# A mixture-of-experts router that reads the residual rows themselves, block by block

## The chip, the cores and the metric

The kernel runs on one core of a Trainium2 chip. The metric is the device time of one execution in microseconds (us). The engines are TensorE (PE, with its weight loads as PEld), VectorE (DVE), ScalarE (ACT), GpSimd (POOL) and SyncE (SP); SP, ACT and POOL issue the DMAs. The trace comes from one profiled execution, with times counted from the start of its span.

## The reference, cut to what matters

One layer of a hybrid encoder on 1024 rows of 1024 channels: a linear-recurrence branch and a differential attention, merged, then cross-attention to 256 memory rows, then a mixture of experts. The change touches the step from the cross-attention's output to the first expert.

```
x = x + MemCrossAttn(RMSNorm(x), RMSNorm(mem))
h = x * rsqrt(mean(x*x) + 1e-6) * norm_ffn                # one row factor, one gain per channel
gp = softmax(h @ w_group + b_group)                       # 4 groups
gval, gidx = top_k(gp, 1)
el = (h @ w_router + b_router)[8 experts of group gidx]   # 32 experts in all
ev, eidx = top_k(el, 2);  ew = softmax(ev) * gval
# each row goes to its two experts: y = (silu(h @ Wg) * (h @ Wu)) @ Wd
x = x + sum over the two experts of ew * y
```

## The kernel before, in words

Rows are worked on in eight blocks of 128 (tb). Matrix products keep float32 accuracy by splitting each operand into a rounded part and a remainder: ScalarE writes the rounded part, VectorE the difference (`split`), and `mm3` issues three matmuls. Weight pieces of 512 KB come from HBM in a fixed order through class `Weights` (L45): `load` issues the DMAs on SP, `split_one` makes the two parts (L97 on ScalarE, L101 on VectorE), `prefetch(n)` allows n pieces in flight ahead, and `after` ties an instruction behind another in the planner's order. All large tiles share one pool of 51 slots of 4 KB per partition (`slot`). PSUM has four one-bank tiles (`bank`) and two two-bank tiles (`bank2`), eight banks in all.

The memory attention runs as a list of steps written by hand, `SEQ` (L1226), one letter and a block or pair each: P, T, S, A, O and M make queries, scores, probabilities and their products with the memory values; C (L1004) is the output projection into PSUM; N (L1020) adds it to x, starts x's write to the output, squares and sums the row on ScalarE (L1027), lets POOL make the row factor (a power of -0.5), multiplies x by factor and gain on VectorE (L1037, tile n3) and writes the normalised row to DRAM (h3_d) from ScalarE's queue. R (L1044) transposes a block of n3 with PE and splits it, two PSUM tiles of four transposes each. L (L1058) multiplies two blocks at once, 256 columns, with the router weights `wrs` (36 logits as a rounded part and a remainder side by side, 72 columns), and ScalarE adds the bias. l (L1070) transposes the logits back, adding the two halves by the matrix id2, and VectorE copies them to SBUF. r and q are the two halves of `st_route` (L1116): r picks group and experts into one-hot rows `ohf` and a mask `mb`; q counts each row's rank among the rows of its expert with PE (prk), makes the gate weights, and then the values and rank one-hots. f is a call of `prefetch`. The list ends with C7 N7 R6 f4 l2 R7 q1 L3 l3 r2 q2; r2 and q2 route blocks 4 to 7. `rt` (L1080) packs small router tiles into shared slots of 1024 numbers.

After the list, PE multiplies one-hots by values into a table of row numbers (pTi) and one of gate weights (pTw), 96 places for each expert (L1280). `table` (L1287) converts row numbers to int32 (idx, L1289) on VectorE; POOL gathers the 96 rows of the first expert from h3_d by an indirect DMA (L1301, tile xe); they are transposed (pxe) and the expert's matmuls (pgu, py) begin. Each of the 32 experts takes twelve weight pieces and scatters its result by an indirect DMA that adds to the output. Before the first gather four weight pieces are split.

A planner that runs a timeline model decides each engine's order of instructions from program order and dependencies.

Of the kernel before, what the change touches and what calls it, by code (L numbers as in the profile page):

```python
# [20 lines left out]
T = 1024  # L21
# [110 lines left out]
def block_kernel(ctx, tc, a):  # L132
# [13 lines left out]
    def slot(name, dt=F32, shape=(P, 1024)):  # L146
        return S.tile(list(shape), dt, tag="s", name=name)

    def bank(name, dt=F32, shape=(P, 512)):
        return pb1.tile(list(shape), dt, tag="b1", name=name)  # L150
# [4 lines left out]
    def f(x):  # L155
        return x.bitcast(F32)
# [53 lines left out]
    rowt = slot("row")  # L210
    row = rowt[:, 0:NROW]
    nc.gpsimd.dma_start(row, a["row"].to_broadcast([P, NROW]))
    posi = cp.tile([P, NB], I32, name="posi")
    nc.gpsimd.dma_start(posi, a["pos"])
    ident = cp.tile([P, P], F32, name="ident")
# [8 lines left out]
    def rstd_of(ss, n, cnt, name):  # L224

        t = sm.tile([P, 16], F32, tag="rs0", name=name + "m")
        r = sm.tile([P, 16], F32, tag="rs1", name=name + "r")
        G.tensor_scalar(t[:, :n], ss, 1.0 / cnt, EPS, op0=OP.mult, op1=OP.add)
        G.tensor_tensor(r[:, :n], t[:, :n], negh[:, :n], op=OP.pow)
        return r  # L230
# [96 lines left out]
    def split(src, h, l):  # L327
        A.activation(h, src, AF.Copy)
        V.tensor_tensor(l, src, f(h), op=OP.subtract)  # L329
# [571 lines left out]
    wr = slot("wr", F32, (P, 8, 36))  # L901
    wrs = slot("wrs", F32R, (P, 8, 72))
    nc.sync.dma_start(wr, a["w_r"])
    A.activation(wrs[:, :, 0:36], wr, AF.Copy)
    V.tensor_tensor(wrs[:, :, 36:72], wr, f(wrs[:, :, 0:36]), op=OP.subtract)

# [111 lines left out]
        return ps if tb >= NB - HN else [both]  # L1018

    def st_N(tb, ps):  # L1020
        x, t = x1[tb], slot(f"n3_{tb}")
        ss = sm.tile([P, 16], F32, tag="ss", name=f"n3_{tb}s")
        n = len(ps)
        parts = [slice(i * D // n, (i + 1) * D // n) for i in range(n)]
        for i, c in enumerate(parts):
            V.tensor_tensor(x[:, c], x[:, c], ps[i], op=OP.add)
            A.activation(t[:, c], x[:, c], AF.Square, accum_out=ss[:, i:i + 1])  # L1027
        nc.scalar.dma_start(a["out"][tb * P:(tb + 1) * P, :], x)
        if n == 2:
            m, r = (sm.tile([P, 16], F32, tag=f"rs{i}", name=f"n3_{tb}r{i}") for i in range(2))  # L1030
            G.tensor_scalar(ss[:, 0:1], ss[:, 0:1], 1.0, D * EPS, op0=OP.mult, op1=OP.add)
            G.tensor_scalar(m[:, 0:1], ss[:, 1:2], ss[:, 0:1], 1.0 / D, op0=OP.add, op1=OP.mult)
            G.tensor_tensor(r[:, 0:1], m[:, 0:1], negh[:, 0:1], op=OP.pow)
        else:
            r = rstd_of(ss[:, 0:1], 1, D, f"n3_{tb}")
        for c in parts:
            V.scalar_tensor_tensor(t[:, c], x[:, c], r[:, 0:1], gffn[:, c], op0=OP.mult, op1=OP.mult)  # L1037
        h3[tb] = t
        nc.scalar.dma_start(h3_d[tb * P:(tb + 1) * P, :], t)
        x1[tb] = None  # L1040

    h3T, lgT = {}, {}

    def st_R(tb):  # L1044

        src = h3.pop(tb)
        c = slice((tb % 2) * P, (tb % 2) * P + P)
        for kq in range(2):
            ps = bank(f"ph3T{tb}_{kq}", F32, (P, 4, P))
            for kk_ in range(4):  # L1050
                k = 4 * kq + kk_
                E.transpose(ps[:, kk_, :], src[:, k * P:(k + 1) * P], ident)  # L1052
            if tb % 2 == 0:
                h3T[tb // 2, kq] = [slot(f"h3T{tb}_{kq}_{i}", F32R, (P, 4, 256)) for i in range(2)]
            t = h3T[tb // 2, kq]
            split(ps, t[0][:, :, c], t[1][:, :, c])

    def st_L(g):  # L1058

        pl = bank(f"plog{g}", F32, (P, 256))[0:72]  # L1060
        for k in range(8):
            t = h3T[g, k // 4]
            for i in range(2):
                W.last = E.matmul(pl, wrs[:, k, :], t[i][:, k % 4, :], start=k + i == 0, stop=k + i == 8)  # L1064
            if k % 4 == 3:
                del h3T[g, k // 4]
        lgT[g] = slot(f"lgT{g}", F32, (P, 256))[0:72]
        A.activation(lgT[g], pl, AF.Identity, bias=vec[0:72, C_BR:C_BR + 1])

    def st_l(g):  # L1070
        src = lgT.pop(g)
        pt = bank(f"plgT{g}", F32, (P, 2, 36))
        for j in range(2):
            W.last = E.matmul(pt[:, j, :], src[:, j * P:(j + 1) * P], id2, start=True, stop=True)  # L1074
        V.tensor_copy(lg[:, 2 * g:2 * g + 2, :], pt)


    rpool = {}
# [1 line left out]
    def rt(name, *shape, dt=F32):  # L1080

        n = math.prod(shape)
        if dt not in rpool or rpool[dt][1] + n > 1024:
            rpool[dt] = [slot(name, dt), 0]
        t, o = rpool[dt]
        rpool[dt][1] = o + n
        v = t[:, o:o + n]
        if len(shape) > 1:
            names = "abcd"[:len(shape)]
            v = v.rearrange(f"p ({' '.join(names)}) -> p {' '.join(names)}", **dict(zip(names, shape)))  # L1090
        return v
# [13 lines left out]
    V.memset(onesb, 1.0)  # L1105
    ohf = rt("ohf", 2, NB, 32)
    mb = cp.tile([P, NB, 32], BF, name="mb")
    lgf = rt("lg", NB * 36)
    lg = lgf.rearrange("p (a b) -> p a b", a=NB)
    rk, ew, ewl = rt("rk", 2, NB), rt("ew", 2, NB), rt("ewl", 2, NB)  # L1110
    ewh = sm.tile([P, 2, NB], F32R, name="ewh", bufs=1)
# [4 lines left out]
    def st_route(b0, n2):  # L1116
# [51 lines left out]
        for t in range(n2 - 1):  # L1168
            E.matmul(prk[:, t + 1:, :], onesb, mb[:, b0 + t:b0 + t + 1, :].to_broadcast([P, n2 - 1 - t, 32]),
                     start=False, stop=t == n2 - 2)  # L1170

        V.tensor_reduce(sg, gd, axis=AX.X, op=OP.add)
        V.reciprocal(gval, sg)
        V.tensor_tensor(m2, m2, m1, op=OP.subtract)
        A.activation(m2, m2, AF.Exp)
        V.tensor_scalar(dn, m2, 1.0, None, op0=OP.add)
        V.reciprocal(dn, dn)
        V.tensor_tensor(ew[:, 0, bs], dn, gval, op=OP.mult)
        V.tensor_tensor(ew[:, 1, bs], ew[:, 0, bs], m2, op=OP.mult)
        V.tensor_copy(ewh[:, :, bs], ew[:, :, bs])  # L1180
        V.tensor_tensor(ewl[:, :, bs], ew[:, :, bs], f(ewh[:, :, bs]), op=OP.subtract)
        va = rt(f"vals{b0}", 2, n2, 3, 32, dt=F32R)
        oh = rt(f"ohs{b0}", 2, n2, CAP, dt=F32R)

        def value(i, c):
            V.tensor_tensor(va[:, :, :, i, :], ohf[:, :, bs], c[:, :, bs, None].to_broadcast([P, 2, n2, 32]),  # L1186
                            op=OP.mult)
# [6 lines left out]
        for k in range(2):  # L1194
            V.tensor_tensor(oh[:, k], slots[:, None, :].to_broadcast([P, n2, CAP]),  # L1195
                            rk[:, k, bs, None].to_broadcast([P, n2, CAP]), op=OP.is_equal)
        value(1, f(ewh))
        value(2, ewl)
        coded.append([(oh[:, k, t, :], va[:, k, t]) for k in range(2) for t in range(n2)])
# [8 lines left out]
    for hf in range(2):  # L1208
        w = W.take(4)
        for tb in range(NB):  # L1210
# [11 lines left out]

    wcq, wco = W.take(4), None
    NG_ = NB // 2
    PF = 12,20,28,36,41
    SEQ = ("P0 T0 P1 T1 S0 S1 P2 P3 O00 O01 O02 T2 O03 T3 M00 M01 C0 A2 S2 S3 N0 C1 N1 P4 O10 O11 P5 "  # L1226
# [3 lines left out]
    done = set()  # L1230
    routes = [st_route(0, 2), st_route(2, 2), st_route(4, 4)]
    pco = {}
    for op in SEQ.split():
        kind, n = op[0], int(op[1])
        if kind == "P":
            st_P(n)
            if n == NB - 1:
                wcq = None
        elif kind == "T":
            st_T(n)  # L1240
        elif kind == "S":
            st_S(n)
        elif kind == "A":
            st_A(n)
        elif kind == "O":
            st_O(n, (int(op[2]),))
        elif kind == "M":
            st_M(n, int(op[2]))
        elif kind == "C":
            if wco is None:  # L1250
                wco = W.take(4)
                W.split_ahead = 0
            pco[n] = st_C(n)
            if n % 2 == 1 and n - 1 in done or n % 2 == 0 and n + 1 in done:
                del om[n // 2]
            done.add(n)
        elif kind == "N":
            st_N(n, pco.pop(n))
        elif kind == "R":
            st_R(n)  # L1260
        elif kind == "L":
            st_L(n)
        elif kind == "l":
            st_l(n)
        elif kind == "w":
            for _ in range(n):
                W.split_one()
        elif kind == "f":
            W.prefetch(PF[n])
        else:  # L1270
            last = W.last
            next(routes[n])
# [13 lines left out]

    def table(code, parts, w_, ix):  # L1287

        V.tensor_scalar(ix, code, 2.0 * T, None, op0=OP.add)  # L1289
        V.tensor_copy(w_, parts[:, 0])  # L1290
        V.tensor_tensor(w_, w_, parts[:, 1], op=OP.add)

    wts = cp.tile([P, 32], F32, name="wts")[0:CAP]
    idx = cp.tile([P, 32], I32, name="idx")[0:CAP]
    table(pTi, pTw, wts, idx)

    xe = slot("xe")[0:CAP]
    G.memset(xe, 0.0)
# [223 lines left out]
```

## Time and profile before

| | us |
|---|---|
| median of 3 runs (lowest, highest) | 1950.39 (1950.25, 1954.46) |
| the profiled execution | 1948.1 |
| its span | 1946.3 |
| PE busy | 1868.9 (96%) |
| DVE busy | 1296.6 (67%) |
| ACT busy | 1103.5 (57%) |
| POOL busy | 327.8 (17%) |

A busy share is an average over the span. The page's row of 40 slices shows that PE is at nine tenths or more in nearly all of them, except the first, the last and the one that begins at 1314 us, between routing and experts. The granted clock of TensorE over the whole run is 0.987 of full speed. The weight DMAs of the experts fill the DMA engines from about 1370 us to the end.

### The profile page before, as it was taken

What the parts mean: (1) busy time and instruction counts of PE and PEld (TensorE: products, weight loads), DVE (VectorE), ACT (ScalarE), POOL (GpSimd) and SP (SyncE); (2) the same over time, 40 slices, a digit from 0 to 9 for tenths busy, and PEclk for the clock granted to TensorE, in tenths of its full rate; (3) what the DMA queues carried; (4) which work ended last, traced back from release to release, by engine and by line L of the source; (5) the groups of instructions that cost most, each with busy time, mean ns of one, the idle gap of its engine ahead of it and who ended that gap; (6) DMA issues with size and microseconds to landing.
All of it is one profiled execution on the core that took longest, in us unless ns stands there. A gap on an engine that the chain in (4) does not pass through costs nothing. (4 is left out here: it accounts for less than half of the span.)

```text
span 1946.3 us, 25814 instructions
## 1 busy us (share of the span) xinstructions
PE 1868.9 (96%) x9214; PEld 1491.7 (77%) x9214; DVE 1296.6 (67%) x1766; ACT 1103.5 (57%) x1631; POOL 327.8 (17%) x432
## 2 busy tenths in 40 slices
PE   6999999999999999899999999996999999999996
PEld 5888888888888888778888887875777777777664
DVE  5222324677777758887444425675899999999985
ACT  5233324555555546876212215452888888888885
POOL 2144430122222221100000001111111111111110
PEclk9999999999999999999999999997999999999998
DMA  5222244433333121225322401177999999999996
GB/s 201 86 87 87 87 134 137 125 108 107 111 118 120 55 101 57 71 90 187 108 77 86 187 22 65 56 281 272 322 355 346 337 349 358 353 348 338 348 367 218
DMA packets 115027, 353.40 MB, mean 182 GB/s; under 512 B 14864, under 2 KB 28304, under 8 KB 114896
## 3 DMA queue, kind: packets, MB, share of 16 engines
q1 hardware_dynamic: 102992, 322.11, 46.9%
q0 software_dynamic: 7296, 17.04, 3.8%
q10 hardware_dynamic: 4608, 12.58, 1.6%
q8 instruction: 73, 1.20, 0.2%
q14 instruction: 58, 0.48, 0.1%
HBM read 311.82 MB, written 48.23 MB: 185 GB/s over the span
## 5 line engine op out<-in xcount | busy, mean ns | idle before, releaser
L101 DVE TENSOR_TENSOR wl<-wraw,wh 128x1024 fp32r<-128x1024 f32 x480 | 576.9, 1227 | 123.7 <-ACT wh L97 111.7
L97 ACT ACTIVATE wh<-wraw 128x1024 fp32r<-128x1024 f32 x480 | 496.3, 1057 | 113.0 <-PE pgu L161 15.9
L160 PE MATMUL pgu<-wl,xeh 128*96 128x512 f32 x512 | 203.7, 398 | 1.0 <-DVE wl L101 1.0
L159 PE MATMUL pgu<-wh,xeh 128*96 128x512 f32 x512 | 203.7, 398 | 0.3 <-ACT wh L97 0.3
L161 PE MATMUL pgu<-wh,xel 128*96 128x512 f32 x512 | 201.2, 393 | 0.0
L505 ACT ACTIVATE p<-pS,st 128x256 f32<-128x256 f32 (+7 forms) x128 | 94.9, 747 | 103.3 <-DVE st L498 51.7
L159 PE MATMUL pga<-hH,wh 128*128 128x512 f32 x320 | 127.4, 398 | 2.5 <-DVE wT L539 2.5
L160 PE MATMUL pga<-hL,wh 128*128 128x512 f32 x320 | 126.0, 394 | 0.0
L161 PE MATMUL pga<-hH,wl 128*128 128x512 f32 x320 | 125.5, 392 | 0.0
L160 PEld LDWEIGHTS pgu<-wl,xeh 128*96 128x96 f32 x512 | 82.9, 162 | 43.5 <-DVE wl L101 12.5
L159 PEld LDWEIGHTS pgu<-wh,xeh 128*96 128x96 f32 x512 | 83.0, 162 | 33.8 <-ACT wh L97 0.5
L161 PEld LDWEIGHTS pgu<-wh,xel 128*96 128x96 f32 x512 | 82.9, 162 | 33.4 <-DVE xel L329 0.2
L1351 POOL DMA_INDIRECT out<-y,idx x32 | 46.4, 1451 | 357.8 <-ACT y L1350 352.9
L514 POOL TENSOR_SCALAR p<-p,st 128x128 f32<-128x128 f32 (+3 forms) x64 | 55.0, 860 | 305.2 <-DVE st L513 159.4
L160 PE MATMUL py<-wl,ah 128*96 128x512 f32 x256 | 101.7, 397 | 0.3 <-DVE wl L101 0.2
L161 PE MATMUL py<-wh,ah 128*96 128x512 f32 x256 | 100.4, 392 | 0.0
L159 PE MATMUL pqk<-wh,hH 128*128 128x512 f32 x256 | 100.3, 392 | 0.0
L161 PE MATMUL pqk<-wh,hL 128*128 128x512 f32 x256 | 100.2, 391 | 0.0
L160 PE MATMUL pqk<-wl,hH 128*128 128x512 f32 x256 | 99.7, 389 | 0.0
L375 ACT ACTIVATE qk<-pT,gq 128x512 f32<-128x512 f32 x32 | 20.2, 686 | 106.8 <-PE pT L374 93.9
L159 PE MATMUL py<-wh,ah 128*96 128x512 f32 x256 | 80.0, 393 | 0.3 <-ACT wh L97 0.3
L493 PE MATMUL pS<-kH,qS 128*128 128x512 f32 (+2 forms) x192 | 69.5, 365 | 5.2 <-ACT p L505 5.2
(527 smaller groups left out, 4415.8 us busy)
## 6 DMA issues: line engine op xcount, KB each, us to landing
wraw<-in_w_gu SPq DMA_DIRECT2D x256, 512.0 KB
wraw<-in_w_dn SPq DMA_DIRECT2D x128, 512.0 KB
wraw<-in_w_cm SPq DMA_DIRECT2D x32, 512.0 KB
x<-in_x SPq DMA_DIRECT2D x16, 512.0 KB
wraw<-in_w_qk SPq DMA_DIRECT2D x32, 256.0 KB
qk_d<-qk SPq DMA_DIRECT2D x32, 256.0 KB
qr<-qk_d SPq DMA_DIRECT2D x32, 256.0 KB
kr<-qk_d SPq DMA_DIRECT2D x32, 256.0 KB
```

The source lines that it names most:

```text
L97: ins = nc.scalar.activation(h, raw, AF.Copy)
L101: nc.vector.tensor_sub(l, raw, h.bitcast(F32))
L159: W.seen(E.matmul(out, lh, rh, start=start, stop=False))
L160: E.matmul(out, lh, rl, start=False, stop=False)
L161: E.matmul(out, ll, rh, start=False, stop=stop)
L375: A.activation(out[i][:, :, c], pt, AF.Copy, scale=gq[:, i:i + 1])
L493: E.matmul(ps[:, o:o + c], lhs, kh_[h, m][:, o:o + c], start=True, stop=False)
L505: A.activation(p[:, :n], ps[:, :n], AF.Exp, bias=mx[:, m:m + 1], accum_out=ls[:, m:m + 1])
L514: G.tensor_scalar(pp[1][:, :n], pp[1][:, :n], rl[:, 1:2], 0.0, op0=OP.mult, op1=OP.add)
L1351: G.indirect_dma_start(out=a["out"][:, :], out_offset=bass.IndirectOffsetOnAxis(ap=dest, axis=0), in_=y, in_offset=None, bounds_check=T - ...
```

## The change

R transposes x itself, as soon as the projection is added, and the channel gains are multiplied into the router weights once, early on; for that a column layout of the gains is read at the start by a POOL DMA. L works on one block of 128 columns, without bias. l multiplies the transposed logits by the row factor and adds the bias row (`brow`, made once by a transpose). N no longer makes the normalised row: a new step H does, for the gather alone, with row factors kept in `r3`. The squares of N go into the projection's own PSUM tile, not into n3. In q the rank part comes ahead of the gate weights. The weight splits in front of the experts are ordered behind the row-number conversion (`W.anchor`). Before the list of steps, a gather of 96 numbers that are all out of bounds is issued, which moves no row. SEQ has the new steps; L and l stand per block, C7 (the last projection) is now followed by l5, H6, N7, q1, L6, R7, l6, L7, H7, l7, r2, f4, q2.

```diff
+    gcol = cp.tile([P, 8], F32, name="gcol")
+    with nc.allow_non_contiguous_dma(reason="1024 gains, one per channel"):
+        nc.gpsimd.dma_start(gcol, a["nffn"].rearrange("o (k p) -> p (o k)", p=P))
...
+    V.tensor_tensor(wr, wr, gcol[:, :, None].to_broadcast([P, 8, 36]), op=OP.mult)
...
     def st_N(tb, ps):
-        x, t = x1[tb], slot(f"n3_{tb}")
+        x = x1[tb]
...
-            A.activation(t[:, c], x[:, c], AF.Square, accum_out=ss[:, i:i + 1])
+            A.activation(ps[i], x[:, c], AF.Square, accum_out=ss[:, i:i + 1])
...
-            m, r = (sm.tile([P, 16], F32, tag=f"rs{i}", name=f"n3_{tb}r{i}") for i in range(2))
+            m = sm.tile([P, 16], F32, tag="rs0", name=f"n3_{tb}r0")
...
-            G.tensor_tensor(r[:, 0:1], m[:, 0:1], negh[:, 0:1], op=OP.pow)
+            G.tensor_tensor(r3[:, tb:tb + 1], m[:, 0:1], negh[:, 0:1], op=OP.pow)
...
-            r = rstd_of(ss[:, 0:1], 1, D, f"n3_{tb}")
-        for c in parts:
-            V.scalar_tensor_tensor(t[:, c], x[:, c], r[:, 0:1], gffn[:, c], op0=OP.mult, op1=OP.mult)
-        h3[tb] = t
+            m = sm.tile([P, 16], F32, tag="rs0", name=f"n3_{tb}r0")
+            G.tensor_scalar(m[:, 0:1], ss[:, 0:1], 1.0 / D, EPS, op0=OP.mult, op1=OP.add)
+            G.tensor_tensor(r3[:, tb:tb + 1], m[:, 0:1], negh[:, 0:1], op=OP.pow)
+    uses = [0] * NB
+    def used(tb):
+        uses[tb] += 1
+        if uses[tb] == 2:
+            x1[tb] = None
+    def st_H(tb):
+        t = slot(f"n3_{tb}")
+        V.scalar_tensor_tensor(t, x1[tb], r3[:, tb:tb + 1], gffn, op0=OP.mult, op1=OP.mult)
...
-        x1[tb] = None
-    h3T, lgT = {}, {}
+        used(tb)
+    xT = {}
...
     def st_R(tb):
...
-        src = h3.pop(tb)
-        c = slice((tb % 2) * P, (tb % 2) * P + P)
...
-            ps = bank(f"ph3T{tb}_{kq}", F32, (P, 4, P))
+            ps = bank(f"pxT{tb}_{kq}", F32, (P, 4, P))
...
-                E.transpose(ps[:, kk_, :], src[:, k * P:(k + 1) * P], ident)
-            if tb % 2 == 0:
-                h3T[tb // 2, kq] = [slot(f"h3T{tb}_{kq}_{i}", F32R, (P, 4, 256)) for i in range(2)]
-            t = h3T[tb // 2, kq]
-            split(ps, t[0][:, :, c], t[1][:, :, c])
-    def st_L(g):
-        pl = bank(f"plog{g}", F32, (P, 256))[0:72]
+                E.transpose(ps[:, kk_, :], x1[tb][:, k * P:(k + 1) * P], ident)
+            t = xT[tb, kq] = slot(f"xT{tb}_{kq}", F32R, (P, 2, 4, P))
+            split(ps, t[:, 0], t[:, 1])
+        used(tb)
+    def st_L(tb):
+        pl = bank(f"plog{tb}", F32, (P, P))[0:72]
         for k in range(8):
-            t = h3T[g, k // 4]
+            t = xT[tb, k // 4]
...
-                W.last = E.matmul(pl, wrs[:, k, :], t[i][:, k % 4, :], start=k + i == 0, stop=k + i == 8)
+                W.last = E.matmul(pl, wrs[:, k, :], t[:, i, k % 4, :], start=k + i == 0, stop=k + i == 8)
...
-                del h3T[g, k // 4]
-        lgT[g] = slot(f"lgT{g}", F32, (P, 256))[0:72]
-        A.activation(lgT[g], pl, AF.Identity, bias=vec[0:72, C_BR:C_BR + 1])
-    def st_l(g):
-        src = lgT.pop(g)
-        pt = bank(f"plgT{g}", F32, (P, 2, 36))
-        for j in range(2):
-            W.last = E.matmul(pt[:, j, :], src[:, j * P:(j + 1) * P], id2, start=True, stop=True)
-        V.tensor_copy(lg[:, 2 * g:2 * g + 2, :], pt)
+                del xT[tb, k // 4]
+        lgT[tb] = slot(f"lgT{tb}", F32, (P, P))[0:72]
+        A.activation(lgT[tb], pl, AF.Copy)
+    lgT = {}
+    def st_l(tb):
+        pt = bank(f"plgT{tb}", F32, (P, 36))
+        W.last = E.matmul(pt, lgT.pop(tb), id2, start=True, stop=True)
+        V.scalar_tensor_tensor(lg[:, tb, :], pt, r3[:, tb:tb + 1], brow, op0=OP.mult, op1=OP.add)
...
-    lgf = rt("lg", NB * 36)
+    lgf, brow, r3 = rt("lg", NB * 36), rt("brow", 36), rt("r3", NB)
+    pbr = bank("pbr")
+    E.transpose(pbr[:, 0:P], vec[:, C_BR:C_BR + 1].to_broadcast([P, P]), ident)
+    V.tensor_copy(brow, pbr[:, 0:36])
+    del pbr
...
+        va = rt(f"vals{b0}", 2, n2, 3, 32, dt=F32R)
+        oh = rt(f"ohs{b0}", 2, n2, CAP, dt=F32R)
+        def value(i, c):
+            V.tensor_tensor(va[:, :, :, i, :], ohf[:, :, bs], c[:, :, bs, None].to_broadcast([P, 2, n2, 32]),
+                            op=OP.mult)
+        value(0, dcode)
+        rtmp = tt(2, n2, 32)
+        for k in range(2):
+            V.tensor_tensor(rtmp[:, k], ohf[:, k, bs], prk, op=OP.mult)
+        V.tensor_reduce(rk[:, :, bs], rtmp, axis=AX.X, op=OP.add)
+        for k in range(2):
+            V.tensor_tensor(oh[:, k], slots[:, None, :].to_broadcast([P, n2, CAP]),
+                            rk[:, k, bs, None].to_broadcast([P, n2, CAP]), op=OP.is_equal)
...
+    idx = cp.tile([P, 32], I32, name="idx")[0:CAP]
+    V.memset(idx[:, 0:1], 2 * T)
+    nil = slot("nil", F32, (P, NVEC))[0:CAP]
+    G.memset(nil, 0.0)
+    G.indirect_dma_start(out=nil, out_offset=None, in_=a["vec"][:, :],
+                         in_offset=bass.IndirectOffsetOnAxis(ap=idx[:, 0:1], axis=0), bounds_check=P - 1,
+                         oob_is_err=False)
+    del nil
...
-    SEQ = ("P0 T0 P1 T1 S0 S1 P2 P3 O00 O01 O02 T2 O03 T3 M00 M01 C0 A2 S2 S3 N0 C1 N1 P4 O10 O11 P5 "
-           "O12 O13 T5 M10 M11 T4 A3 S5 R0 C2 R1 L0 S4 l0 r0 C3 N2 N3 P6 O20 O21 P7 T6 O22 O23 M21 f0 "
-           "f1 T7 S6 M20 q0 R2 S7 R3 O30 L1 C4 O32 N4 l1 r1 R4 O33 O31 C5 N5 f2 M31 M30 f3 C6 N6 R5 "
-           "L2 C7 N7 R6 f4 l2 R7 q1 L3 l3 r2 q2 ")
+    SEQ = ("P0 T0 P1 T1 S0 S1 P2 P3 O00 O01 O02 T2 O03 T3 M00 M01 C0 A2 S2 S3 N0 C1 H0 N1 P4 O10 O11 P5 H1 "
+           "O12 O13 T5 M10 M11 T4 A3 S5 R0 C2 R1 L0 S4 L1 l0 l1 r0 C3 N2 N3 H2 P6 O20 H3 O21 P7 T6 O22 O23 M21 f0 "
+           "f1 T7 S6 M20 q0 R2 S7 R3 O30 L2 C4 L3 O32 N4 l2 l3 r1 R4 O33 O31 H4 C5 N5 f2 L4 M31 M30 R5 H5 f3 C6 N6 "
+           "L5 l4 R6 C7 l5 H6 N7 q1 L6 R7 l6 L7 H7 l7 r2 f4 q2 ")
...
+        elif kind == "H":
+            st_H(n)
...
     def table(code, parts, w_, ix):
...
-        V.tensor_scalar(ix, code, 2.0 * T, None, op0=OP.add)
+        ins = V.tensor_scalar(ix, code, 2.0 * T, None, op0=OP.add)
...
+        return ins
...
-    idx = cp.tile([P, 32], I32, name="idx")[0:CAP]
-    table(pTi, pTw, wts, idx)
+    W.anchor, W.want = table(pTi, pTw, wts, idx), False
...
```

## Rows read from the trace of the kernel before

**Rows 1.** Stretches: length, busy of each engine, granted clock, DMA share, GB/s.
```profile
1250.00:1300.00 50.00, 47.33 (x287) 40.58 (x286) 36.11 (x82) 24.35 (x63) 5.33 (x9) 1.00 0.61 236
1300.00:1310.00 10.00, 7.72 (x44) 6.93 (x43) 6.81 (x20) 4.49 (x10) 0.75 (x2) 0.88 0.42 131
...
1345.00:1362.00 17.00, 8.14 (x37) 6.42 (x37) 10.01 (x22) 4.79 (x7) 3.49 (x2) 0.50 0.18 54
...
1400.00:1850.00 450.00, 449.94 (x2131) 317.02 (x2130) 411.69 (x408) 384.93 (x455) 61.55 (x50) 1.00 0.99 348
1850.00:1931.00 81.00, 78.75 (x362) 53.72 (x360) 69.37 (x68) 65.90 (x79) 9.68 (x7) 1.00 0.93 342
```

**Rows 2.** Timeline of DVE around the hole: start, us, line, operation.
```profile
1328.55 0.69 DVE L1026 TENSOR_TENSOR x<-x,pco 128x512 f32<-128x512 f32 x1 [3.02 <-PE pco L161]
...
1331.37 1.42 DVE L1037 SCALAR_TENSOR_TENSOR n<-x,n_7r,gffn 128x512 f32<-128x512 f32 x2 [0.81 <-POOL n_7r L1033]
...
1339.48 0.23 DVE L1075 COPY im<-plgT 128x72 f32<-128x72 f32 x1 [1.67 <-PE plgT L1074]
...
1344.57 0.29 DVE L1162 TENSOR_TENSOR mb<-im 128x128 bf16<-128x128 f32 x1
...
1345.90 0.42 DVE L1193 TENSOR_REDUCE im<-route 128x8 f32<-128x256 f32 x1
...
1346.64 1.01 DVE L1195 TENSOR_TENSOR ohs<-im 128x384 fp32r<-128x384 f32 x2
...
1347.92 2.35 DVE L101 TENSOR_TENSOR wl<-wraw,wh 128x1024 fp32r<-128x1024 f32 x2
1350.19 0.18 DVE L1289 TENSOR_SCALAR idx<-pTi 96x32 int32<-96x32 f32 x1
```

**Rows 3.** Timelines of PE and ACT; in brackets the wait before.
```profile
1306.88 1.37 PE L1052 MATMUL ph3T<-ident,n 128*128 128x128 f32 x8 [2.28 <-DVE n L1037]
...
1320.53 0.60 PE L1052 MATMUL ph3T<-ident,n 128*128 128x128 f32 x4
1320.88 1.19 PE L1064 MATMUL plog<-h3T,wrs 128*72 128x256 f32 x8
...
1334.58 3.67 PE L1064 MATMUL plog<-h3T,wrs 128*72 128x256 f32 x16
1338.81 0.64 PE L1074 MATMUL plgT<-im,lgT 72*128 72x36 f32 x4 [0.56 <-ACT lgT L1068]
...
1339.82 0.50 PE L1281 MATMUL pTw<-vals 128*96 128x64 f32 x4
1340.16 0.49 PE L1281 MATMUL pTi<-vals 128*96 128x32 f32 x4
...
1347.25 1.46 PE L1281 MATMUL pTi<-vals,ohs 128*96 128x32 f32 x8 [1.91 <-DVE ohs L1195]
...
1334.59 0.60 ACT L328 ACTIVATE h3T<-ph3T 128x512 fp32r<-128x512 f32 x1 [0.67 <-PE ph3T L1052]
1338.29 0.47 ACT L1068 ACTIVATE lgT<-plog,vec 72x256 f32<-72x256 f32 x1 [3.10 <-PE plog L1064]
```

**Rows 4.** Chain of waits at two gathers; POOL's timeline at the start.
```profile
1351.24 5.59 DMA xe<-h_d,idx
...
1358.76 4.04 DMA xe<-h_d,idx
...
2.09 0.59 POOL L214 DMA_DIRECT2D posi<-in_pos  x1
...
5.63 0.19 POOL L228 TENSOR_SCALAR n_0m<-n_0s 128x1 f32<-128x1 f32 x1 [1.44 <-ACT n_0j L235]
```

**Rows 5.** Timelines of DVE and ACT: block 2's add and its square.
```profile
1252.04 1.22 DVE L1026 TENSOR_TENSOR x<-x,pco 128x1024 f32<-128x1024 f32 x1 [0.58 <-PE pco L161]
...
1267.38 1.06 ACT L1027 ACTIVATE n<-x 128x1024 f32<-128x1024 f32 x1
```

More of the change, by code (lines that the diff above doesn't have):

```diff
@@ L1170, in st_route @@
                      start=False, stop=t == n2 - 2)
[L1172 to L1181, printed above, removed]
         va = rt(f"vals{b0}", 2, n2, 3, 32, dt=F32R)
@@ L1196, in st_route @@
                             rk[:, k, bs, None].to_broadcast([P, n2, CAP]), op=OP.is_equal)
+        V.tensor_reduce(sg, gd, axis=AX.X, op=OP.add)
+        V.reciprocal(gval, sg)
+        V.tensor_tensor(m2, m2, m1, op=OP.subtract)
+        A.activation(m2, m2, AF.Exp)
+        V.tensor_scalar(dn, m2, 1.0, None, op0=OP.add)
+        V.reciprocal(dn, dn)
+        V.tensor_tensor(ew[:, 0, bs], dn, gval, op=OP.mult)
+        V.tensor_tensor(ew[:, 1, bs], ew[:, 0, bs], m2, op=OP.mult)
+        V.tensor_copy(ewh[:, :, bs], ew[:, :, bs])
+        V.tensor_tensor(ewl[:, :, bs], ew[:, :, bs], f(ewh[:, :, bs]), op=OP.subtract)
         value(1, f(ewh))
```

## The prediction

> **What bounds the kernel now.** I read the stretches by stage first, then the timelines of PE and DVE around the one hole in PE's work, then the chain of waits across it. The stretches show three regimes [rows 1]. Up to the last output projection of the memory attention, near 1328 us, PE is the bound (47.33 of 50 us at full clock). From 1345 to 1362 us nearly everything stands: PE 8.14 of 17 us at clock 0.50, the lower of its two levels (1.2 GHz), DMA share 0.18. From 1362 us the experts run with PE full and the DMA share at 0.99; from 1850 us PE has 78.75 of 81 us, so the weight stream's lead is then about used up. The hole is a serial chain: DVE adds the last half of block 7 to x until 1329.24; its square sum, row factor and normalised row follow (until 1332.79), then transposes, splits, 16 logit matmuls, a copy and a transpose back; the logits lie in SBUF at 1339.71; routing ends in the rank one-hots at 1347.65; the row numbers start at 1350.19 [rows 2]; the first gather lands 5.59 us after its issue at 1351.24 [rows 4]. What shortens this chain moves the whole expert stage forward; what adds PE work before 1328 us moves it back.
>
> **The change part by part.** I subtract from the profiled execution: span 1946.3 us, run 1948.1. The three timed runs have median 1950.39, 2.3 above it, so the same difference is taken from the median.
>
> *Router on x.* From the end of the last x add to the logits in SBUF took 1339.71 - 1329.24 = 10.47 us [rows 2]. Afterwards the square sum, row factor and normalised row leave this path, the first four transposes can run while C7's second half is still multiplying, and block 6 is no longer in the same logit group. What remains: four transposes (0.60 at full clock [rows 3], twice that at half; I take 0.8), a ScalarE split of 0.60 and the DVE one (0.69, as the 128x512 add), eight logit matmuls, the copy (0.47 for 256 columns; 0.4), one transpose back (half of 0.64), the DVE fused step 0.23 and seven handoffs of 0.03. A 256-column logit matmul took 3.67/16 = 0.23 at half clock; with 128 columns I take 0.13, so 1.0 for eight (bounds 0.5 and 1.8). Sum 4.2, so 6.3 less. The row factor of block 7 is needed only at the last step, when POOL has long made it. Against that: the normalised rows still have to be made for the gather (1.42 each in two halves [rows 2]), and they, with the rank work of blocks 2 and 3 (about 2 us), can now stand in DVE's queue before the split. DVE had idle stretches of up to 3.02 us before the x adds [rows 2], enough for most of it. Bounds 0 and 4.8; I take 1.0. Net 5.3 less. The block rows' writes go out from ScalarE's queue some 8 us before the gather needs them; hidden.
>
> *Ranks first.* From the mask (ends 1344.86) to the one-hots' end is 2.79 us, with weight steps between the reduce (ends 1346.32) and the one-hots' start (1346.64) [rows 2]. Moving them behind saves 0.32 and a little before the reduce: 0.4 (0 to 0.8).
>
> *Row numbers ahead of weight splits.* The eight row-number matmuls end at 1347.25 + 1.46 = 1348.71 [rows 3]; the conversion waits behind two weight splits on DVE (2.35 us from 1347.92) until 1350.19 [rows 2]. With the splits ordered behind it: 1.4 less (0 to 1.4). The four splits then cost DVE about 4 x 1.2 = 4.8 us while the gather is under way (0.87 us to issue and 4.04 to land [rows 4]); just hidden, and each one that is not costs 1.2.
>
> *Early gather.* The first gather took 5.59 us to land, the next 4.04 [rows 4]. If the difference belongs to the first use of this operation, it is paid near 1180 us, where POOL only makes row factors: 1.5 less (0 to 1.55). Its clearing memset needs a slot of the shared pool, and row factors of the query stand behind it on POOL; slots are short only later, so I charge nothing (1.5 if not).
>
> *PE work before 1328 us.* Block 6's transposes now come before C7 ends: 8 x 0.09 = 0.7 (four start 0.35 apart from the next group [rows 3]). Logits of six blocks: 96 matmuls of 128 columns in place of 48 of 256. The 256-column ones took 0.23 at half clock, so 0.12 at full [rows 3], 5.8 in all. For 128 columns the nearest row is the 64-column one, (1340.16 - 1339.82)/4 = 0.085 [rows 3], which is weight-load time for 96 columns; 72 are loaded here, so I take 0.07: 6.7, or +0.9 (bounds: 0.06 each, nothing; 0.23 each, a 512-column price, +16). Transposes back and the bias transpose +0.6. Together +2.2. Given back: PE waited 2.28 us for block 4's normalised row [rows 3], which starts about when x is ready, so reading x saves about 1.4 (that row's own step); and the clock fell in that stretch (0.88 over 1300 to 1310 us [rows 1]), which without the wait may not happen (0 to 1.7; I take 0.8). Net 0 (bounds -2.5 and +18).
>
> *Square into PSUM.* The output projection's bank is now held until ScalarE has squared the row. For block 2 the add ended at 1253.26 and the square at 1268.44 [rows 5], so 15 us with today's order. ScalarE needs no free slot for it any more and can go sooner, and PE has query projections ready instead. I take 0.3; the upper end is a rival below. The Trainium skill (ScalarE: Activation LUTs, "Step-by-step: what each stage is for") calls PSUM the faster destination for ScalarE, but only useful if TensorE doesn't need most of PSUM; here all eight banks are in use, so its caveat speaks against this edit. Weighed as a gain of latency it would give nothing on the path.
>
> *Start of the kernel.* The gain column is a POOL DMA of 1024 single elements ahead of the row factors. The small one there took 0.59 us to issue, and POOL then idled 1.44 before the first row factor [rows 4]. Between one such issue (hidden) and eight (4.7 - 1.4 = 3.3, if all of that delays the first product) I take 0.2. The Trainium skill (DMA: Bandwidth & Descriptors, "Rules for kernel authors") says a non-contiguous last dimension becomes one descriptor per element and should be rearranged; the trace of before has no such transfer. If issue time went with descriptors, the sum would be nearer its upper end.
>
> *Slots and stream.* Small router tiles fill 1004 of a slot's 1024 floats; 44 more open a second slot for the rest of the program, so of 51 one fewer holds a weight piece. The last five prefetched pieces also start only behind the last transpose back (f4 moved), and the first splits come closer to the experts. At DMA share 0.99 a lost piece of 512 KB costs 1.5 us at the 348 GB/s of [rows 1]. Bounds 0 and 4.5 (a piece, and 3 us of lead); I take 0.8.
>
> Gains 5.3 + 0.4 + 1.4 + 1.5 = 8.6, costs 0 + 0.3 + 0.2 + 0.8 = 1.3: net 7.3. 1948.1 - 7.3 = 1940.8 in a profiled execution; against the median 1950.4 - 7.3 = 1943.1 us.
>
> **The rivals.** *The weight stream binds.* For: DMA share 0.99 and a PE short of full after 1850 us [rows 1]. Then lost lead comes back as waits at the end and only about 2.5 us remain: 1948. Against: the stream's idle 17 us are the same hole, and it restarts when the experts free slots, so it moves along.
> *More goes than I count.* If the clock's fall and the waits for normalised rows go fully (1.0 and 0.9 more), DVE's collisions vanish (1.0) and slots freed earlier keep the stream's lead (0.8 and up to 2 of late waits), some 5 more: 1938.
> *Held PSUM banks, on the slower side.* Place: the output projections of blocks 0 to 3, whose two-bank tiles the following scores and projections take in turn. Price: the delay of the square behind the add, 15.2 us for block 2 with today's order [rows 5]. It decides where PE stands for more than 7.3 us of it, about half; for all of it, 1943.1 + 15.2 = 1958. For: [rows 5]. Against: PE shows hardly any wait for banks now, and the order is planned anew with the hold known. It is also what the caveat quoted from the Trainium skill would make of the time.
> *Short matmuls cost as much as long ones.* At 0.23 each, +16 before the hole and about 1.5 in it: 1961. Against: the 0.085 us of 64 columns [rows 3].
> *The early gather does nothing:* 1.5 of the gain stays out: 1944.6, inside the forecast's range.
>
> **How the numbers follow.** Forecast 0.55 (own range 1938 to 1948), stream 0.15, more 0.16, banks 0.10, short matmuls 0.04. A measurement of this kernel can tell about 0.3% from no change, 5.9 us here: faster means below 1944.5. Of the forecast's 0.55 I give 0.40 to that and 0.15 to within; "more" is faster, 0.16; stream 0.15 and a fifth of the banks 0.02 are within; the rest, 0.08 and 0.04, slower. Faster 0.56, same 0.32, slower 0.12. The range 1934 to 1952.5 holds the forecast, the stream and most of "more", and leaves out the banks at their price and the short matmuls.
>
> **What would show it.** Right: from the last x add to the last block's logits 5 to 6 us; the row-number conversion within 0.2 us of the last row-number matmul, no weight split before it; the first expert gather landing in about 4 us and one early POOL gather; 128 logit matmuls 0.06 to 0.09 us apart at full clock; PE from 1362 us on as full as now, ending about 7 us sooner. Wrong: PE waits on ScalarE's squares before block 3's projection; logit matmuls 0.2 apart at full clock; normalised rows on DVE between the last x add and the split; more PE waits for weights after 1850 us.

## The result, and the profile after

The changed kernel takes 2027.13 us (median of 4 runs, 2023.18 to 2031.75), the kernel before 1952.23 us beside it: 1.0398 times as long, 95% interval 1.0379 to 1.0417. Forecast were 1943.1 us and a range of 1934 to 1952.5. Its profiled execution has a span of 2023.8 us and took 2025.6.

Stretches of the changed kernel, as in [rows 1]:

```profile
1250.00:1300.00 50.00, 44.79 (x284) 38.24 (x283) 36.44 (x83) 22.85 (x59) 6.63 (x12) 1.00 0.56 211
1300.00:1310.00 10.00, 10.00 (x72) 8.65 (x72) 5.04 (x7) 5.96 (x16) 0.75 (x2) 1.00 0.40 159
1345.00:1362.00 17.00, 7.70 (x55) 7.24 (x55) 13.93 (x48) 4.70 (x7) 2.31 (x2) 0.54 0.57 201
1400.00:1850.00 450.00, 402.59 (x1836) 270.45 (x1836) 353.72 (x358) 330.15 (x392) 51.62 (x43) 0.99 0.97 331
1850.00:1931.00 81.00, 74.62 (x344) 50.37 (x343) 65.75 (x65) 62.15 (x75) 9.63 (x8) 1.00 0.97 341
```

The loss is in the experts: PE is busy 402.59 of 450 us where it had been full, and PE, DVE, ScalarE and the DMA rate all fall together, so none of them looks like the bound. The first expert product starts at 1362.6 (1358.4 before), the last at 2006.8 (1929.9): 644.2 us against 571.5. The two products in the timeline of PE, after and then before:

```profile
1362.56 0.74 PE L159 MATMUL pgu<-wh,xeh 128*96 128x512 f32 x1
...
2006.80 0.40 PE L161 MATMUL py<-wh,ah 128*96 128x512 f32 x1
```

```profile
1358.42 0.74 PE L159 MATMUL pgu<-wh,xeh 128*96 128x512 f32 x1
...
1929.92 0.40 PE L161 MATMUL py<-wh,ah 128*96 128x512 f32 x1
```

What the experts wait for stands in the page's costliest groups, of the changed kernel:

```profile
L101 DVE TENSOR_TENSOR wl<-wraw,wh 128x1024 fp32r<-128x1024 f32 x480 | 575.5, 1226 | 194.4 <-ACT wh L97 128.9
L97 ACT ACTIVATE wh<-wraw 128x1024 fp32r<-128x1024 f32 x480 | 489.9, 1055 | 153.5 <-DVE wl L101 79.4
L160 PE MATMUL pgu<-wl,xeh 128*96 128x512 f32 x512 | 206.8, 404 | 40.1 <-DVE wl L101 40.1
```

and of the kernel before:

```profile
L101 DVE TENSOR_TENSOR wl<-wraw,wh 128x1024 fp32r<-128x1024 f32 x480 | 576.9, 1227 | 123.7 <-ACT wh L97 111.7
L97 ACT ACTIVATE wh<-wraw 128x1024 fp32r<-128x1024 f32 x480 | 496.3, 1057 | 113.0 <-PE pgu L161 15.9
```

PE waits for DVE's weight part, ScalarE for DVE too, and DVE's own idle time grew by 71 us while each of its operations stayed at 1.23 us. DVE's waits between 1400 and 1850 us (line, releaser, total, times, longest), after:

```profile
DVE wl L101 <- DMA out<-y,idx: 40.6, 16, 3.1
DVE wl L101 <- ACT wh L97: 37.5, 66, 2.1
DVE wl L101 <- issue: 8.6, 3, 2.9
```

The first row does not exist in the trace of before. A weight split has no data from the scatter of an expert's output y: it waits because it writes into y's buffer. One expert, timelines of ScalarE, POOL and DVE, then PE:

```profile
1463.93 1.26 ACT L1378 ACTIVATE y<-py,wts 96x512 f32<-96x512 f32 x2
...
1465.47 1.42 POOL L1379 DMA_INDIRECT out<-y,idx  x1 [13.91 <-ACT y L1378]
...
1470.05 1.22 DVE L101 TENSOR_TENSOR wl<-wraw,wh 128x1024 fp32r<-128x1024 f32 x1
1474.24 1.23 DVE L101 TENSOR_TENSOR wl<-wraw,wh 128x1024 fp32r<-128x1024 f32 x1 [2.97 <-DMA out<-y,idx]
...
1495.03 1.23 DVE L101 TENSOR_TENSOR wl<-wraw,wh 128x1024 fp32r<-128x1024 f32 x1 [2.99 <-DMA out<-y,idx]
...
1475.52 0.47 PE L160 MATMUL pgu<-wl,xeh 128*96 128x512 f32 x1 [1.64 <-DVE wl L101]
```

y is written until 1465.2, its scatter is issued from 1465.47 and lands at 1474.16 (8.3 us is the median of such a landing), and the split that inherits the buffer starts at 1474.24: it stood at the head of DVE's queue for 2.97 us with everything behind it. The same happens 20.8 us later.

The hole did get shorter, but began later. Timelines after, DVE, PE and POOL, as in [rows 2 to 4]:

```profile
1339.54 0.68 DVE L1031 TENSOR_TENSOR x<-x,pco 128x512 f32<-128x512 f32 x1
...
1346.31 0.26 DVE L1088 SCALAR_TENSOR_TENSOR im<-plgT,im 128x36 f32<-128x36 f32 x1 [0.34 <-PE plgT L1087]
...
1351.42 0.29 DVE L1179 TENSOR_TENSOR mb<-im 128x128 bf16<-128x128 f32 x1
...
1353.49 1.02 DVE L1201 TENSOR_TENSOR ohs<-im 128x384 fp32r<-128x384 f32 x2
...
1355.60 0.19 DVE L1317 TENSOR_SCALAR idx<-pTi 96x32 int32<-96x32 f32 x1 [0.75 <-PE pTi L1309]
...
1334.70 0.50 PE L159 MATMUL pco<-wh,om 128*128 128x512 f32 x1 [1.59 <-ACT pco L1032]
...
1340.97 1.23 PE L1077 MATMUL plog<-xT,wrs 128*72 128x128 f32 x16 [1.61 <-DVE xT L332]
1342.03 1.06 PE L1066 MATMUL pxT<-ident,x 128*128 128x128 f32 x8
...
1354.10 1.46 PE L1309 MATMUL pTi<-vals,ohs 128*96 128x32 f32 x8 [1.91 <-DVE ohs L1201]
...
1361.08 1.54 PE L1339 MATMUL pxe<-ident,xe 96*128 96x96 f32 x8 [4.22 <-DMA xe<-h_d,idx]
...
1177.57 1.96 POOL L1247 DMA_INDIRECT nil<-in_vec,idx  x1 [0.29 <-POOL nil L1246]
```

C7's last product starts 9.2 us later than before (1337.3 against 1328.1); from there to the first expert product it takes 25.2 us instead of 30.3.

### The profile page after: what moved, and what is told of

It is laid out like the page before. It is cut to its first block, busy times and chain, and to the rows that moved or that the text cites. A ratio compares the mean times of both kernels' runs of the same rounds, so it can differ in the third digit from the quotient of the medians.

```text
span 2023.8 us, 25886 instructions
## 1 busy us (share of the span) xinstructions
PE 1889.2 (93%) x9279; PEld 1489.8 (74%) x9279; DVE 1295.7 (64%) x1771; ACT 1100.5 (54%) x1635; POOL 328.5 (16%) x435
## 4 chain that ended last, share of the span: by engine, by line
PE 50%; issue 22%; DMA 14%; DVE 8%; ACT 5%; POOL 1%; POOLq 0%; SPq 0%; ACTq 0%; DVEq 0%
DMA out<-y,idx 12%; PE pqk L160 3%; PE pqk L159 3%; PE pqk L161 3%; PE pga L159 3%; PE pga L160 3%; PE pga L161 3%; PE pya L160 1%; PE pya L161 1%; PE pyr L161 1%; PE pyr L160 1%; PE pyr L159 1%; PE pya L159 1%; PE pv L159 1%; PE pv L160 1%
## 5 line engine op out<-in xcount | busy, mean ns | idle before, releaser
L97 ACT ACTIVATE wh<-wraw 128x1024 fp32r<-128x1024 f32 x480 | 489.9, 1055 | 153.5 <-DVE wl L101 79.4
```

Of the source, the lines that this page charges most:

```text
L97: ins = nc.scalar.activation(h, raw, AF.Copy)
```

## The experiments

One theory and two rivals at first. A, inheritance: the change shifts the list of buffers so that y's passes to wl. By the addresses that the programs give their tiles, y's buffer goes in 27 of 32 experts to the 16th tile taken from the pool after it, a raw piece, in the kernel before, and to the 15th, a low weight part wl, in the changed one. Rivals: B, the lost buffer costs the stream its lead; C, the splits' order behind the row numbers.

**e1, the buffer back.** The 44 floats live in dead columns of the vector table:

```diff
-    lgf, brow, r3 = rt("lg", NB * 36), rt("brow", 36), rt("r3", NB)
+    lgf, brow, r3 = rt("lg", NB * 36), vec[:, 0:36], vec[:, 36:36 + NB]
```

> The changed kernel with its bias row and row factors (44 floats) kept in columns of the vector table that are dead by then, so that the router's small tiles fit one buffer of the shared pool again, as before. Theory A, inheritance: in the changed kernel the buffer of each expert's output y passes to the low weight part wl of a later piece, which DVE must write in its order while y's scatter is still under way (2.97 us of idle at 1474.24, 19.93 us per expert against 17.71). With the buffer back, y's passes to a prefetched raw piece as before. Then 17.7 us per expert and no DVE wait for a scatter; the first expert product still comes at 1362.6 against 1358.4, so 1950.4 + 4.1, about 1954.5 (1951 to 1959). Rival B, one buffer fewer costs the weight stream its lead: also cured here, the same 1954. Rival C, the splits ordered behind the row numbers upset DVE and ScalarE in the experts: nothing changes, about 2027.

1962.55 us, 1.0082 (1.0063 to 1.0101) of before: 0.0316 x 1950 = 62 us of the 78 gone. No DVE wait for a scatter is left, though the scatters still land after 8.2 us. The time is above the expected range: beside 1947.26 us for the kernel before, a loss of 15 us remains where 4 were expected.

**e2, the kernel before with 50 buffers:** `NS = 50`.

> The kernel before with 50 buffers in the shared pool instead of 51, nothing else. Theory A: with 50 the list of buffers passes y's to wl, as in the changed kernel, so 19.9 us per expert: 1950.4 + 32 x 2.2 = 2021 (2014 to 2028), and DVE idle before wl until the scatter. Rival B, lost lead: one piece of 512 KB less, 1.5 us once and some waits at the end, 1952 to 1957, DVE not waiting for scatters. Rival C (the order of splits): 1950 to 1955, as nothing of the order is in it.

2024.26 us, 1.0393 (1.0375 to 1.0411): the whole loss, with nothing of the router in it. DVE's waits, 1400 to 1850 us:

```profile
DVE wl L101 <- ACT wh L97: 38.3, 68, 2.1
DVE wl L101 <- DMA out<-y,idx: 30.6, 11, 3.9
```

These rows leave out some of the waits, which the profile puts down to other releasers. Counted by the landings themselves, over the whole of e2's trace, 25 of the 32 scatters land some 0.08 us before the start of a weight split that DVE had stood idle for, 67 us in all, beside 77 us lost.

**e3, the changed kernel with 36 pieces asked ahead:** `W.load_ahead = 36`.

> The changed kernel with 36 instead of 37 raw pieces asked ahead in the expert stage; it still has one buffer fewer. Theory A: y's buffer now passes to a raw piece again, so 17.7 us per expert and about 1954.5, at most 4.5 more for the lead of the pieces: 1953 to 1960. Rival B: there is one buffer fewer and one piece less asked ahead, so it is at least as slow as the changed kernel: 2027 or more. Rival C: 2027.

1968.26 us, 1.0113 (1.0095 to 1.0131). One buffer fewer than e1 and one piece less ahead, and yet nearly all of the loss is gone: B falls. The buffer itself is worth what is left, about 0.3% or 6 us, and that is barely clear of the noise: the intervals of e1 and e3 overlap, and their profiled executions took 1961.1 and 1960.5 us.

**e4, without the order of the splits:** `table(pTi, pTw, wts, idx)` with no anchor.

> The changed kernel with the weight splits no longer ordered behind the row numbers. Theory A: y's buffer still passes to wl: about 2027, plus up to 1.4 for the row numbers that wait behind two splits again (2024 to 2032). Rival B: the same. Rival C: the loss goes, about 1955.

2035.71 us, 1.0456 (1.0432 to 1.0480): C falls. From C7's last product to the first of the experts it takes 29.2 us instead of 25.2, so this part of the change is worth up to 3.9. The issue of the first expert's gather on POOL, in the kernel before and in the changed one, then in e4 the early gather and the same issue:

```profile
1351.24 2.52 POOL L1301 DMA_INDIRECT xe<-h_d,idx  x1 [10.73 <-DVE idx L1289]
```

```profile
1356.58 1.36 POOL L1329 DMA_INDIRECT xe<-h_d,idx  x1 [9.60 <-DVE idx L1317]
```

```profile
1179.04 1.96 POOL L1247 DMA_INDIRECT nil<-in_vec,idx  x1 [0.29 <-POOL nil L1246]
...
1363.79 2.57 POOL L1329 DMA_INDIRECT xe<-h_d,idx  x1 [11.04 <-DVE idx L1317]
```

So e4 has the early gather, and its first expert gather is as slow as before.

**e5, the kernel before once more.**

> The kernel before, unchanged, for a trace beside the next three. With the buffer back, the changed kernel still took 15 us more than before, of which 7 lie in the expert stage (578.5 us from the first product to the last, against 571.5 in the trace of before). Theory A, the weight stream sets the end of the experts and the 7 us belong to the changed kernel: 571 to 572 here again. Rival D, the 7 us are the difference between two profiled executions: 575 to 579 here.

569.0 us (from 1358.8 to the last product's start at 1927.8): D falls: the kernel before gives 571.5 and 569.0, so the 7 us and more belong to the changed kernel.

**e6, three parts without the router.**

```diff
 # the kernel before, with: rank one-hots ahead of the weights' arithmetic,
+    W.anchor, W.want = table(pTi, pTw, wts, idx), False
 # and the early gather of no row into a small tile
```

> The kernel before with three parts of the change and not the fourth: ranks first, row numbers ahead of the splits, early gather; the router as before. Theory A: nothing changes up to C7, and in the hole the parts bring 0.4 + 1.4 and the 2.7 us by which PE's wait for the first gather fell (6.95 to 4.22): the first expert product 4.5 earlier. If the weight stream restarts with it, 1947.3 - 4.5 = 1943; if not, it takes the gain back as waits after 1780 us: 1947 (rival B). Rival E, the three parts are what slows the kernel outside the buffer question: 1955 or more.

1946.47 us, 0.9993 (0.9978 to 1.0008). In the trace the first expert product comes 2.8 us earlier than in e5 (1356.0) and the last 3.5 earlier; the times can't tell that from nothing. E falls.

**e7, x read for blocks 6 and 7 alone,** on top of e6: a second table of gain-scaled router weights, the last blocks' transposes from x, the gain column as eight more columns of the vector table.

> As the kernel with three parts, and the router reads x for blocks 6 and 7 alone, with a second, gain-scaled table of router weights; blocks 0 to 5 as before, squares into SBUF. Theory A: the 8 us that the changed kernel loses between 1175 us and C7's end come from reading x for all blocks (64 short matmuls more, logits of a block waited for on PE, squares in PSUM), so they stay away, and the hole is 4 to 6 us shorter still than with three parts: 1936 to 1943. Rival F, transposes and logits of the last two blocks cost ahead of C7's end what they save behind it: 1943 to 1947. Rival B, the stream: 1947.

1956.51 us, 1.0052 (1.0034 to 1.0070): a miss. C7's last product starts as in e5 (1329.7), but the hole takes 29.0 us, no less than e5's 29.1, and the experts 576.1.

**e8, squares into SBUF,** on top of e1:

```diff
-            A.activation(ps[i], x[:, c], AF.Square, accum_out=ss[:, i:i + 1])
+            A.activation(sqj[:, c], x[:, c], AF.Square, accum_out=ss[:, i:i + 1])
```

> The changed kernel with the buffer back and the square written to an SBUF buffer instead of the projection's bank. If the held banks are the cause of the 8 us between 1175 us and C7's end: about 1954. If they cost only the one wait that the trace shows (1.59 us before C7's second half): 1961.

1958.38 us, 1.0053 (1.0034 to 1.0072; the interval overlaps with e1's). From the last product of the mixer's output projection to C7's last it takes 155.8 us; with the banks held 159.7 (changed kernel) and 161.1 (e1), in e5 153.2. By these traces held banks cost 4 to 5 us and reading x for all blocks 2.6; but e9 below, with 51 small memsets ahead and the router as before, has 149.7 there, so this stretch moves by as much for other reasons too. The first expert product comes at 1358.8, as in e5; the experts still take 581.3 us against 569.0.

That remainder is the stream. From SP's timeline, the median distance of the 214 to 227 expert pieces that follow each other within 1.1 to 1.5 us is 1.23 us in the kernel before, e5 and e6, and 1.27 in e1, e3, e7 and e8, at a DMA share of 0.99 or 1.00 in all.

**e9 and e10, other places for the tiles** (51 one-column memsets at the start; all buffers taken and given back once), in the kernel before and in e1.

> The kernel before with its 51 buffers all taken and given back once at the start (51 one-column memsets on DVE), so that every tile lies at another address of the pool; who inherits whose buffer in the experts is as before. With the inheritance mended the changed kernel's weight stream still needs 566 to 569 us from its restart to its last piece, against 557 in the kernel before, at the same DMA share of 0.99 and with the same instructions in the expert stage. Rival G, the addresses of the buffers set the stream's rate: 557 becomes something else, up to 569, and the kernel up to 1960. Otherwise: 557 again and 1947, plus up to 3 for the memsets at the start.

> The changed kernel with its buffer back, and all 51 buffers taken and given back once at the start, as in the run beside it. Rival G (addresses): the 566 us of the stream change, down to 557, and the kernel with them, down to 1953. Otherwise: 566 again, 1962 to 1965.

1949.93 us, 1.0011 (0.9993 to 1.0030), pieces 1.23 us apart; and 1960.31, 1.0052 (1.0033 to 1.0071), 1.27 apart. Another place for every tile changes neither number. What was left: in e1, e3, e7, e8 and e10 the small tiles are 32 bytes larger (the gain column, or eight more table columns), so that every buffer begins 32 bytes further on, at 19232 + 4096 n instead of 19200 + 4096 n.

**e11, six pieces in flight,** on top of e6: `W.flying = 6`.

> The kernel with three parts (ranks first, row numbers ahead of the splits, early gather), and six weight pieces in flight at most instead of four. y's buffer passes to a high weight part wh some 4 us later in the order than wl was, so no wait for the scatter is expected. If the stream sets the end and four in flight leave DMA engines unused at times: up to 1% of 554 us, 1940 to 1946. If DMA is full with four: 1946. If more in flight delays each single piece, or gathers and scatters behind them: 1950 or more.

1955.51 us, 1.0030 (1.0020 to 1.0040), though the stream did get faster. The expectation missed a wait: y's buffer passes to a high part wh in 23 experts, and ScalarE waits for scatters there (1400 to 1850 us):

```profile
ACT wh L97 <- DMA out<-y,idx: 5.8, 10, 1.1
```

Stretch 1400 to 1850 us of e11, then e6:

```profile
1400.00:1850.00 450.00, 443.06 (x2087) 308.54 (x2086) 400.21 (x397) 371.93 (x447) 60.50 (x49) 1.00 1.01 366
```

```profile
1400.00:1850.00 450.00, 450.00 (x2136) 317.46 (x2135) 412.69 (x407) 386.23 (x458) 61.95 (x50) 1.00 1.00 354
```

**e12, 32 bytes in the kernel before:**

```diff
+    pad = cp.tile([P, 8], F32, name="pad")
+    G.memset(pad[:, 0:1], 0.0)
```

> The kernel before with one more small tile of 32 bytes ahead of the pool, so that all 51 buffers begin at 19232 instead of 19200 bytes; the tile is written once and not used. Theory H, the start of the buffers sets the rate of the weight transfers: pieces 1.27 us apart instead of 1.23, the stream 564 to 569 us instead of 557, the kernel 1953 to 1959. Rival: it was something of the router on x: 1.23, 557 and 1947 to 1950.

1961.27 us, 1.0061 (1.0040 to 1.0082), pieces 1.27 us apart. The order of instructions on every engine is that of the kernel before, but for the one memset, and a split takes 1.23 us in both: the place of the tiles alone does it.

**e13, all parts mended:** e8, with the gain column in dead columns of the vector table and loaded ahead of its use.

```diff
-    gcol = cp.tile([P, 8], F32, name="gcol")
+    gcol = vec[:, 44:52]
```

> All parts of the change, with the buffer back, squares into SBUF, and the gain column kept in columns of the vector table that are dead by then and loaded just ahead of its use, so that the buffers begin at 19200 again. Theory H: pieces 1.23 us apart, the stream 557 us; the first expert product came at 1358.8 with these squares, as in the kernel before: 1945 to 1949. Rival: 1.27, 566 and 1957 to 1960 as without the last edit.

1946.18 us, 0.9987 (0.9975 to 0.9999), pieces 1.23 us apart. This is the only version whose interval lies below the kernel before, by 2.5 us, but only just, and it overlaps with e6's, where the router is as before. The traces don't show a gain of the router on x: e13's first expert product starts at 1358.9 and its last at 1927.7, e5's at 1358.8 and 1927.8, e6's at 1356.0 and 1924.3. Four pieces in a row on SP's queue in e13 (three distances in 3.98 - 0.33 us), then in e12 (4.16 - 0.33):

```profile
1461.59 3.98 SPq L78 DMA_DIRECT2D wraw<-in_w_dn  x4
```

```profile
1479.22 4.16 SPq L78 DMA_DIRECT2D wraw<-in_w_gu  x4
```

Stretch 1400 to 1850 us of e13, then e12: PE is full again only where the stream is at 351 GB/s.

```profile
1400.00:1850.00 450.00, 450.00 (x2133) 317.42 (x2132) 412.93 (x408) 386.68 (x458) 62.46 (x51) 1.00 0.99 351
```

```profile
1400.00:1850.00 450.00, 444.26 (x2085) 309.56 (x2084) 403.86 (x400) 378.15 (x448) 61.73 (x50) 1.00 0.99 342
```

**e14 and e15, six in flight and 38 ahead,** on top of e6 and of e13.

> The kernel with three parts, six weight pieces in flight and 38 asked ahead: y's buffer passes to a raw piece again (with 37 it went to wh, and ScalarE waited 5.8 us for scatters). If the inheritance was what six in flight lost by: PE full in the experts, 32 x 17.71 = 567 us from the first product, 1941 to 1946. If not: 1955 as with 37.

> All parts mended as in the run of that name, with six in flight and 38 asked ahead. If PE is the bound of the experts then: as all parts mended, less at most 4 us of late waits for weights: 1942 to 1948. If y's buffer or gathers hold it up: 1953 or more.

1979.97 us, 1.0166 (1.0149 to 1.0183), and 1982.67, 1.0179 (1.0162 to 1.0196): neither brought a gain, and e14 is far above both of its values. y's buffer goes to a raw piece in 24 experts, so inheritance by y isn't it. PE's waits in e14 from 1400 us on:

```profile
PE pgu L160 <- DVE wl L101: 10.9, 28, 1.6
PE py L160 <- DVE wl L101: 9.1, 26, 0.6
PE pgu L159 <- ACT wh L97: 3.0, 1, 3.0
```

The raw pieces are early and the splits late; what holds the splits back was not settled. One thing they share with the other slow versions: the changed kernel, e2 and e4 (50 - 37) and e14 and e15 (51 - 38) leave 13 buffers beside the raw pieces asked ahead, all others 14. With four in flight, then, y's heir and this number always changed together; that the heir costs most there rests on the scatters' landings in the traces. That a missing buffer can also cost in another way, e14 and e15 leave open.

## Why the prediction was wrong

The step that failed is *Slots and stream*. It saw that 44 floats open a second buffer and that one of 51 is lost, and priced that as lost bytes, at 0.8 us (bounds 0 and 4.5). The bytes cost about 6 us, barely clear of the noise (e3 against e1). What it left out is that with 50 buffers the rotation changes: a buffer that a slow scatter still reads passes from a raw piece, whose load SP issues, to a split that DVE must do in its order. That is 62 us by e1's ratio; e2's gives 77 for a buffer fewer, 67 of them seen as DVE's waits for scatters. The forecast sign "PE from 1362 us on as full as now" failed with it: 402.59 of 450 us. No rival had it; "weight stream binds" looked at the stream's bytes only.

A second effect was in no term at all: the 32 bytes of the gain column move all buffers, and the weight transfers then follow each other 3% further apart (1.27 for 1.23 us). e12 prices it at 0.61% or 12 us, e13 against e8 at 0.66% or 13. The stream of the kernel before has next to no reserve for this: PE already falls short after 1850 us [rows 1].

*Router on x.* From the last x add's end to the logits: 1346.57 - 1340.22 = 6.35 us against a forecast of 5.2 and 10.47 before, but that add itself started 1.8 us after the end of C7's last product, behind block 6's normalised row, a split and routing work on DVE: the collision that was charged 1.0. The first transposes of block 7, too, did not run under C7's second half, as was foreseen: by the order of the steps (L6 ahead of R7) they are the eight from 1342.03 on, behind block 6's sixteen logit matmuls, which had waited 1.61 us for that block's split. From C7's end (1328.5 and 1337.7) to the logits it is 8.9 us for 11.2: a gain of 2.3, not 5.3. In e13 little of it is left (from the add's end at 1332.96 to 1342.80 it is 9.8 us, from C7's end 10.6), and e7's hole is no shorter either. *Square into PSUM*, charged 0.3, costs 4 to 5 by the traces, of which PE's wait of 1.59 us for ScalarE before C7's second half (the row at 1334.70) is one part; the rival of the held banks, and with it the caveat quoted from the Trainium skill (ScalarE: Activation LUTs, "Step-by-step: what each stage is for"), was right in kind and below its price of 15. *PE work before 1328 us*, charged 0: 2.6, inside its bounds; the short logit matmuls came 0.065 us apart at full clock (0.07 taken).

*Ranks first* brought nothing: from the mask's end to the one-hots' end 2.80 us against 2.79. *Row numbers ahead of weight splits* held: the conversion starts 0.04 us after the last row-number matmul (1355.56), 1.4 sooner. *Early gather* came out near its size, but not for its reason: from the end of the conversion to the first transpose of gathered rows it takes 5.29 us instead of 6.60, so 1.3 against 1.5, and POOL's issue fell from 2.52 to 1.36 (the prediction's 0.87 us "to issue" is the time up to its start). But e4, with the early gather and without the order of the splits, has 6.47 and 2.57, so the early gather alone brings nothing, and the first use of the operation is not what the first expert gather pays for. No run has the order alone; why the issue is shorter with it stays open. That the sum of these two terms fits (e6's hole is 2.6 us shorter than e5's) is luck in part. *Start*: the first products start between 72.5 and 76.6 us whatever the kernel, and no cost of the gain column's load is seen.

With both accidents and the squares mended the change gives 2.5 us (0.2 to 4.9) where 7.3 were forecast, and the traces show none of it to come from the router on x.

## What to carry to other kernels

Before a small tile is added to a kernel whose pool of buffers rotates, look up who inherits each buffer that a slow DMA still reads: the price is not the lost buffer but the queue in which its heir stands. Compare the start addresses of the buffers too, when a kernel lives by its weight stream. And test such accidents on the kernel before, with nothing else changed: e2 and e12 settled in one run each what the changed kernel could only suggest.

## What was not expected of the hardware

Loads of 512 KB into buffers that begin 32 bytes further on follow each other 1.27 instead of 1.23 us apart, 413 against 426 GB/s. 19200 is a multiple of 256 and 19232 of 32 only; which step between matters, and why, stays open. The Trainium skill (SBUF — State Buffer, "Operand start alignment") gives the rule for such addresses as one of legality, not of speed; here the start has a price in time (e12).

With six pieces in flight the core's DMA moved 366 GB/s over 450 us. The Trainium skill (DMA: Bandwidth & Descriptors, "Specifications") gives about 358 GB/s as the limit from HBM per core, half of a stack's 716; this run, on one core, is a little above it with its scatters and gathers, the weight pieces alone being 338 GB/s (290 of 512 KB).
